# New memory layout for the output projection and the SwiGLU stages, earlier first weights, and squares per tile

## The chip, the cores and the metric

The kernel runs on one core of one Trainium2 chip. The metric is the device time of one execution in microseconds (us). Its median over three executions was 3259.71 us.

## The reference, cut to what matters

The program is one decoder layer over 2048 positions of width 1024, in float32. The parts that matter here come after attention:

```python
merged = g_a * (y_a @ w_proj_a) + g_b * (y_b @ w_proj_b)
x = x + merged @ w_out
h = rms_norm(x, norm_ffn)
x = x + (silu(h @ w_gate) * (h @ w_up)) @ w_down
return rms_norm(x, final_norm)
```

The inner width of the SwiGLU is 2816. `rms_norm` divides each position by the root of its mean square, so it needs a sum of squares over all 1024 features of a position before the first value can be scaled.

## The kernel before

Features lie on the 128 partitions, positions along the free dimension. Every float32 product is made of three fp32r matmuls (`mm3`, lines 161 to 163): a tile is split into a rounded high part (ACT, line 153) and the rest as a low part (DVE or POOL, line 154), and high·high, high·low and low·high are added up in PSUM. A matmul has 128x128 weights and 512 moving columns.

After attention come three stages, each with its own pools, opened one after the other. A pool sits on the left or the right side of the memory, and a tile that lies where an older tile lay waits for the last reader of the older one.

**Stage 3** goes over four groups `j` of 512 positions. For each of eight feature tiles `m`, `project` makes `y_a @ w_proj_a` (PE tile `ppr`, weights `wpr` loaded by SP and split to `wph`, `wpl`), multiplied with a gate (`sg`); the branch b part `mb` is loaded and added by POOL, and split to `mgh` and `mgl`. Then eight rows of the output projection follow (PE tile `po`, line 1070 on, weights `woh`, `wol` which are loaded as `wor` and split once, in j = 0), each of 24 matmuls. DVE adds the residual in `xo`, POOL stores it to `d_x1`, ACT squares it, DVE adds the squares up. `stats` turns the sum into a scale and POOL stores that to `d_rb`. `prep_b` reads `d_x1` and `d_rb` back, makes the right-hand combinations of the seven-product (Strassen) scheme for one pair of feature tiles, and stores them to `d_b`; those of product 1 are kept in `fb0`. It is called at four (j, m) rows.

**Stage 4**, gate and up, makes for two halves of 1024 positions and eleven pairs `p` of weight blocks seven products `i`, in the order 1, 4, 5, 7, 3, 2, 6, each for gate and for up, each of 12 matmuls (PE tile `pgu`). `w_unit` combines the raw weights `fraw` (POOL, tile `cmb`) and splits them (`wfh`, `wfl`); the moving tiles are `fh`, `fl`, read back from `d_b` in the first pass (`load_b`). `store_acts` writes the activations to `d_a`, `prep_down` the combined down weights to `d_w`.

**Stage 5**, down, goes over products 7, 4, 5, 1, 2, 3, 6, each over two halves of the positions and eleven `p`, with four PSUM banks (PE tile `pdn`, 132 matmuls of 512 columns per half). `unit` loads a raw tile and splits it to `uh`, `ul`. `load_acc` loads the residual from `d_x1`; DVE adds each product into it (line 1271). After product 2 and product 6 `final` squares eight tiles one after the other (ACT and DVE), sums over the partitions (`pss`), takes the root, spreads the scale over 512 columns (`dgh`, `dgl`, `pbc`, `rb`), scales eight tiles (line 1244) and stores them.

The order of the instructions on an engine comes from a scheduler that takes the code in program order with a model of durations; within an engine and within the queue of DMAs that it issues, everything goes in that order. SP issues nearly all loads and stores.

## Time and profile before

| what | us |
|---|---|
| median of three executions (lowest 3253.27, highest 3263.06) | 3259.71 |
| the profiled execution | 3251.75 |
| its span | 3250.0 |
| TensorE (PE) busy in the span | 3091.9, 95% |
| VectorE (DVE) busy | 2310.0, 71% |
| ScalarE (ACT) busy | 1433.5, 44% |
| GpSimd (POOL) busy | 1269.9, 39% |

Idle PE time is what there is to gain, since PE is busy nearly everywhere. A row of the waits names who was idle, on which line, and which engine ended that wait. The granted clock (PEclk) is the level that the throttle gave TensorE; 1.00 is 2.4 GHz, and one half is 1.2 GHz.

### The profile page before, as it was taken

How to read it: one execution, taken by the hardware profiler on the slowest of the kernel's cores; microseconds unless marked ns; L12 is line 12 of the kernel's file. 1: busy time of each engine (PE TensorE's matmuls, PEld its weight loads, DVE VectorE, ACT ScalarE, POOL GpSimd, SP SyncE). 2: the span in 40 equal slices, each digit the busy share in tenths (PEclk: the TensorE clock that was granted, in tenths of full speed). 3: DMA queues.
4: the chain of work that ended last, by engine and by line, in shares of the span. 5: the costliest groups of instructions: out<-in, count | busy, mean ns of one | idle time of the engine just before them, and what ended most of it. 6: DMA issues, size and time to landing. Idle time of an engine off the chain costs nothing.

```text
span 3250.0 us, 42942 instructions
## 1 busy us (share of the span) xinstructions
PE 3091.9 (95%) x14434; PEld 2520.4 (78%) x14434; DVE 2310.0 (71%) x4121; ACT 1433.5 (44%) x2687; POOL 1269.9 (39%) x1250
## 2 busy tenths in 40 slices
PE   7999999999899999999899989999999999799998
PEld 6877777777788787888688767888888888688886
DVE  7369998999742888888654757777877666455575
ACT  6434535452344777767421134333533333333342
POOL 3644323352554324233354333333355555331220
PEclk9999999999999999999899989999999999899999
DMA  6424332332553222222466733443644444754453
GB/s 201 113 71 134 106 100 97 119 106 91 205 161 118 77 69 89 73 69 70 149 213 190 272 130 117 140 139 140 230 156 175 156 165 146 262 162 143 135 189 104
DMA packets 249631, 453.32 MB, mean 139 GB/s; under 512 B 35264, under 2 KB 73920, under 8 KB 249280
## 3 DMA queue, kind: packets, MB, share of 16 engines
q1 hardware_dynamic: 231104, 390.78, 36.7%
q0 software_dynamic: 18304, 59.78, 4.9%
q8 instruction: 113, 1.85, 0.2%
q14 instruction: 110, 0.90, 0.1%
HBM read 299.54 MB, written 150.93 MB: 139 GB/s over the span
## 4 chain that ended last, share of the span: by engine, by line
PE 69%; DVE 17%; issue 5%; DMA 3%; ACT 3%; POOL 1%; SPq 0%; DVEq 0%; ACTq 0%; POOLq 0%
PE pgu L162 9%; PE pgu L161 9%; PE pgu L163 9%; PE pdn L161 4%; PE pdn L162 4%; PE pdn L163 4%; DVE X L489 4%; PE ptp L833 3%; DVE y L532 3%; PE pm L161 2%; PE pm L163 2%; PE pm L162 2%; PE O L840 2%; PE O L841 2%; PE pg L161 1%
## 5 line engine op out<-in xcount | busy, mean ns | idle before, releaser
L972 POOL TENSOR_TENSOR cmb<-fraw 128x512 f32<-128x512 f32 x275 | 399.6, 1467 | 473.7 <-DVE wfl L154 454.2
L161 PE MATMUL pgu<-fh,wfh 128*128 128x512 f32 x1232 | 488.6, 398 | 9.5 <-ACT fh L153 5.7
L162 PE MATMUL pgu<-fl,wfh 128*128 128x512 f32 x1232 | 489.8, 398 | 1.8 <-DVE fl L154 1.8
L163 PE MATMUL pgu<-fh,wfl 128*128 128x512 f32 x1232 | 489.0, 398 | 1.7 <-DVE wfl L154 1.7
L161 PEld LDWEIGHTS pgu<-fh,wfh 128*128 128x128 f32 x1232 | 233.1, 189 | 67.1 <-ACT fh L153 7.0
L162 PEld LDWEIGHTS pgu<-fl,wfh 128*128 128x128 f32 x1232 | 233.6, 190 | 59.2 <-DVE fl L154 3.5
L163 PEld LDWEIGHTS pgu<-fh,wfl 128*128 128x128 f32 x1232 | 233.4, 189 | 58.4 <-DVE wfl L154 2.8
L489 DVE SCALAR_TENSOR_TENSOR X<-rl,wi,X 128x512 f32<-128x512 f32 (+3 forms) x266 | 232.1, 882 | 56.9 <-ACT rl L485 43.8
L154 DVE TENSOR_TENSOR wfl<-cmb,wfh 128x512 fp32r<-128x512 f32 x220 | 187.8, 862 | 107.4 <-ACT wfh L153 107.3
L154 DVE TENSOR_TENSOR ul<-raw,uh 128x512 fp32r<-128x512 f32 x154 | 148.1, 969 | 160.9 <-ACT uh L153 160.7
L153 ACT ACTIVATE wfh<-cmb 128x512 fp32r<-128x512 f32 x220 | 138.3, 631 | 264.9 <-PE pgu L162 181.3
L153 ACT ACTIVATE uh<-raw 128x512 fp32r<-128x512 f32 x231 | 137.9, 627 | 253.6 <-PE pdn L163 133.4
L161 PE MATMUL pdn<-uh 128*128 128x512 f32 x616 | 229.6, 391 | 19.1 <-ACT uh L153 19.1
L162 PE MATMUL pdn<-ul,uh 128*128 128x512 f32 x616 | 240.6, 391 | 0.0
L163 PE MATMUL pdn<-uh,ul 128*128 128x512 f32 x616 | 238.6, 390 | 0.0
L161 PE MATMUL pm<-wh,hT 128*128 128x512 f32 (+1 forms) x576 | 223.0, 391 | 12.2 <-ACT wh L153 4.1
L1140 DVE TENSOR_TENSOR s<-s,pgu 128x512 f32<-128x512 f32 x264 | 175.1, 678 | 78.0 <-PE pgu L163 60.1
L485 ACT ACTIVATE rl<-sc 128x512 f32<-128x512 f32 (+3 forms) x304 | 158.6, 549 | 154.9 <-DVE X L489 85.3
L163 PE MATMUL pm<-wh,lT 128*128 128x512 f32 (+1 forms) x576 | 223.6, 389 | 0.0
L162 PE MATMUL pm<-wl,hT 128*128 128x512 f32 (+1 forms) x576 | 223.2, 388 | 0.4 <-POOL wl L154 0.3
L154 POOL TENSOR_TENSOR ul<-raw,uh 128x512 fp32r<-128x512 f32 x77 | 106.6, 1390 | 283.9 <-ACT uh L153 276.1
L153 ACT ACTIVATE pth<-ptp 128x512 fp32r<-128x512 f32 (+1 forms) x320 | 162.3, 532 | 121.3 <-PE ptp L833 112.2
(314 smaller groups left out, 7769.8 us busy)
## 6 DMA issues: line engine op xcount, KB each, us to landing
raw<-d_a SPq DMA_DIRECT2D x154, 256.0 KB, 2.7
wraw<-in_w_in_dram SPq DMA_DIRECT2D x64, 512.0 KB, 4.4
d_a<-cmb SPq DMA_DIRECT2D x110, 256.0 KB, 2.3
fraw<-in_w_gate_dram SPq DMA_DIRECT2D x22, 1024.0 KB, 4.8
fraw<-in_w_up_dram SPq DMA_DIRECT2D x22, 1024.0 KB, 5.0
d_sg<-zg POOLq DMA_DIRECT2D x64, 256.0 KB, 2.6
sg<-d_sg SPq DMA_DIRECT2D x64, 256.0 KB, 3.6
d_w<-cmb SPq DMA_DIRECT2D x55, 256.0 KB, 2.1
```

The lines of the kernel that those rows point to most:

```text
L153: act.activation(h, src, AF.Copy)
L154: lo.tensor_tensor(l, src, _f(h), op=ALU.subtract)
L161: pe.matmul(out, ah, bh, start=first, stop=False, skip_group_check=onto)
L162: pe.matmul(out, ah, bl, start=False, stop=False, skip_group_check=onto)
L163: pe.matmul(out, al, bh, start=False, stop=last, skip_group_check=onto)
L485: act.activation(r[:, :w], sc[:, :w], AF.Relu)
L489: dve.scalar_tensor_tensor(xs, r[:, :w], wi[:, i, h:h + 1], xs, op0=ALU.mult, op1=ALU.add)
L532: dve.tensor_scalar(y, Xs[p], t[:, p:p + 1], None, op0=ALU.is_ge, op1=ALU.add, accum_out=c[:, p:p + 1])
L833: pe.transpose(pt[:, t * P:(t + 1) * P], out["P"][t, kt // 8][:, (kt % 8) * P:(kt % 8 + 1) * P], ident)
L840: pe.matmul(O[:, cs], V, a[:, cs], start=(kt == 0), stop=False)
L972: eng.tensor_tensor(s, blocks[form[0]], blocks[form[1]], op=form[2])
L1140: dve.tensor_tensor(s[to], s[to], b, op=op)
```

## The change

The pools of the three stages are laid out anew. In stage 3 the weights and work tiles go to the right side and `pr_` to the left, the buffers of `mgh` and `mgl` go from 9 to 8, and those of `prep_b` from 8 to 7 in a pool of their own. Stage 4's raw and split weights (`fr`, `fg`) take the place of `pr_`, `cmb` has 2 buffers instead of 3, and the moving tiles get a pool for each product on the right side. Stage 5's raw tiles and split activations lie where product 1's and its neighbours' moving tiles lay, and its split weights alternate between two pools.

Because of that, the first raw weights of gate and up are loaded inside the output projection of j = 3, and `w_unit` for products 1, 4 and 5 is called at the rows m = 1, 2 and 3 there. `prep_b` moves from (2,1), (2,5), (3,1), (3,4) to (2,1), (2,4), (2,6), (3,0). The store to `d_x1` goes from POOL to ACT. In stage 5 each accumulator is squared when it is complete and the square is added into one `sums` tile, and the last half of product 6 is made in two passes of 256 columns, each with a `final` of its own.

```diff
-    pr_, _ = open_pool("pr", 2, side="right", stack=c3r)
-    pp, _ = open_pool("pp", stack=c3)
-    pw, _ = open_pool("pw", 2, stack=c3)
+    pb_, _ = open_pool("pb", side="right", stack=c3)
+    pw, _ = open_pool("pw", 2, side="right", stack=c3)
+    pp, _ = open_pool("pp", side="right", stack=c3)
+    pr_, _ = open_pool("pr", 2, stack=c3r)
...
-        pl, tag = (fb0, f"{k}") if i == 1 else (fbr, f"{i}_{k}")
-        h = pl.tile([P, 512], F32R, name="fh", tag="fh" + tag)
-        l = pl.tile([P, 512], F32R, name="fl", tag="fl" + tag)
+        h = fbp[i].tile([P, 512], F32R, name="fh", tag=f"fh{k}")
+        l = fbp[i].tile([P, 512], F32R, name="fl", tag=f"fl{k}")
         split(h, l, src, dve)
...
-        return pw.tile([P, 512], dt, name=name, tag="pb3", bufs=8)
+        return pb_.tile([P, 512], dt, name=name, tag="pb3", bufs=7)
...
+    c4 = ExitStack()
+    early = {}
+
+    def cmb(name, dt=F32):
+        return fg.tile([P, 512], dt, name=name, tag="cmb", bufs=2)
+
+    def w_unit(blocks, i):
+
+        src = combine(SA[i], blocks, cmb, pool)
+        h = fg.tile([P, 512], F32R, name="wfh", tag="wfh", bufs=6)
+        l = fg.tile([P, 512], F32R, name="wfl", tag="wfl", bufs=6)
+        split(h, l, src, dve)
+        return h, l
+
+    def load_pair(w, p):
+
+        raw = fr.tile([P, 2, D], F32, name="fraw")
+        sp.dma_start(raw, w[2 * p:2 * p + 2].rearrange("f p c -> p f c"))
+        return {(u, v): raw[:, u, v * 512:(v + 1) * 512] for u in range(2) for v in range(2)}
...
-            h = pw.tile([P, 512], F32R, name="mgh", tag="mgh", bufs=9)
-            l = pw.tile([P, 512], F32R, name="mgl", tag="mgl", bufs=9)
+            h = pw.tile([P, 512], F32R, name="mgh", tag="mgh", bufs=8)
+            l = pw.tile([P, 512], F32R, name="mgl", tag="mgl", bufs=8)
...
+        else:
+            c3r.close()
+            fr, _ = open_pool("fr", 3, stack=c4)
+            fg, _ = open_pool("fg", stack=c4)
+            raws = [load_pair(w, 0) for w in (w_gate, w_up)]
         for m in range(KT):
+            if j == 3 and 1 <= m <= 3:
+                i = ORDER[m - 1]
+                for n, raw in enumerate(raws):
+                    early[n, i] = w_unit(raw, i)
...
-            pool.dma_start(d_x1[m * P:(m + 1) * P, rows], xo)
             sq = st_.tile([P, 512], F32, name="sal") if j == 3 and m == KT - 1 else sq3("sq3")
             act.activation(sq, xo, AF.Square)
+            act.dma_start(d_x1[m * P:(m + 1) * P, rows], xo)
...
-            if (j, m) in ((2, 1), (2, 5), (3, 1), (3, 4)):
-                prep_b(0, {(2, 1): 0, (2, 5): 1, (3, 1): 2, (3, 4): 3}[j, m], pb3, keep=(1,))
+            if (j, m) in ((2, 1), (2, 4), (2, 6), (3, 0)):
+                prep_b(0, {(2, 1): 0, (2, 4): 1, (2, 6): 2, (3, 0): 3}[j, m], pb3, keep=(1,))
...
-    fr, _ = open_pool("fr", 3, side="right", stack=c4)
-    fg, _ = open_pool("fg", side="right", stack=c4)
-    fbr, _ = open_pool("fbr", stack=c4)
     fw, _ = open_pool("fw", 2, stack=c4)
+    for i in ORDER[1:]:
+        fbp[i] = open_pool(f"fb{i}", side="right", stack=c4)[0]
...
-            raws = [load_pair(w, p) for w in (w_gate, w_up)]
+            if half or p:
+                raws = [load_pair(w, p) for w in (w_gate, w_up)]
             grp = [Group(), Group()]
             for i in ORDER:
                 if half == 0 and p == 0 and i != 1:
                     load_b(0, i, tmp)
-                for g, raw in zip(grp, raws):
-                    g.product(i, w_unit(raw, i))
+                for n, (g, raw) in enumerate(zip(grp, raws)):
+                    g.product(i, early.pop((n, i), None) or w_unit(raw, i))
...
+    fx, _ = open_pool("fx", side="right", stack=c5)
+    fu, _ = open_pool("fu", side="right", stack=c5)
+    fv = [open_pool(f"fv{u}", side="right", stack=c5)[0] for u in range(2)]
     fa, _ = open_pool("fa", side="right", stack=c5)
-    fx, _ = open_pool("fx", stack=c5)
+    fy, _ = open_pool("fy", 2, stack=c5)
     QN = KT // 2
...
-    def unit(src, kind, bufs, eng):
-        raw = fx.tile([P, 512], F32, name="raw", tag="raw" + kind, bufs=4)
+    def unit(src, pl, kind, bufs, eng):
+        w = src.shape[-1]
+        raw = fx.tile([P, 512], F32, name="raw", tag="raw" + kind, bufs=4)[:, :w]
         sp.dma_start(raw, src)
-        h = fx.tile([P, 512], F32R, name="uh", tag="h" + kind, bufs=bufs)
-        l = fx.tile([P, 512], F32R, name="ul", tag="l" + kind, bufs=bufs)
-        split(h, l, raw, eng)
-        return h, l
+        hl = pl.tile([P, 2, 512], F32R, name="u" + kind, tag="u" + kind, bufs=bufs)
+        split(hl[:, 0, :w], hl[:, 1, :w], raw, eng)
+        return hl[:, 0, :w], hl[:, 1, :w]
 
...
+    def square(half, n, a, c0, w):
+
+        cs = slice(c0, c0 + w)
+        if (half, n) not in sums:
+            sums[half, n] = fy.tile([P, 512], F32, name="sums", bufs=3)
+            act.activation(sums[half, n][:, cs], a[:, cs], AF.Square)
+            return
+        sq = fy.tile([P, 512], F32, name="sq4", bufs=3)
+        act.activation(sq[:, :w], a[:, cs], AF.Square)
+        dve.tensor_tensor(sums[half, n][:, cs], sq[:, :w], sums[half, n][:, cs], op=ALU.add)
+
...
+    def final(half, n, c0, w):
+
+        cs, nt = slice(c0, c0 + w), w // P
+        sa = sums[half, n][:, cs]
         pss = bank("B", "pss4")
-        for t in range(4):
-            pe.matmul(pss[:, t:t + 1], sa[:, t * P:(t + 1) * P], ones[:, 0:1], start=(t == 0), stop=(t == 3))
-        ss = fx.tile([P, 4], F32, name="ss4")
...
+    DONE = {1: (0, 0), 2: (1, 0), 3: (0, 1), 6: (1, 1)}
     seen = set()
+    nw = 0
     for i in (7, 4, 5, 1, 2, 3, 6):
         wu = []
-        for half in range(2):
-            pms = [bank("A", "pdn") for _ in range(QN)]
+        for half, c0, w in ((0, 0, 512), (1, 0, 512)) if i != 6 else ((0, 0, 512), (1, 0, 256), (1, 256, 256)):
...
-                    wu.append(unit(a_src(i, p), "w", 14, pool))
-                bh, bl = unit(d_a[half, i, p], "a", 4, dve)
+                    wu.append(unit(a_src(i, p), fv[nw // 7 % 2], "w", 7, pool))
+                    nw += 1
+                bh, bl = unit(d_a[half, i, p][:, cs], fu, "a", 4, dve)
...
-                    dve.tensor_tensor(a, a, pm, op=op)
+                    dve.tensor_tensor(a[:, cs], a[:, cs], pm, op=op)
+                    if DONE.get(i) == q:
+                        square(half, q[1], a, c0, w)
             if i in (2, 6):
-                final(half, 0 if i == 2 else 1)
+                final(half, 0 if i == 2 else 1, c0, w)
```

On ACT, at the end of the output projection, the program before has the squares of the last rows and then the first split weights; the names `xo` are the result rows, `wfh` the split weights, `s1` a copy of gate or up:

```order
L1075 ACTIVATE sq3_20213<-xo_20184 128x512
L1075 ACTIVATE sal_20245<-xo_20216 128x512
L153 ACTIVATE wfh_20273<-cmb_20271 128x512
L153 ACTIVATE wfh_20294<-cmb_20292 128x512
L153 ACTIVATE wfh_20337<-fraw_20267 128x512
L153 ACTIVATE wfh_20356<-fraw_20269 128x512
L153 ACTIVATE wfh_20401<-cmb_20399 128x512
L153 ACTIVATE wfh_20423<-cmb_20421 128x512
L153 ACTIVATE wfh_20469<-cmb_20467 128x512
L1125 ACTIVATE s1_20290<-pgu_20277 128x512
```

The changed program:

```order
L153 ACTIVATE wfh_20040<-cmb_20038 128x512
L1103 ACTIVATE sq3_19999<-xo_19971 128x512
L1104 DMA d_x1_99<-xo_19971 128x512
L1103 ACTIVATE sq3_20078<-xo_20050 128x512
L1104 DMA d_x1_99<-xo_20050 128x512
L153 ACTIVATE wfh_20046<-cmb_20044 128x512
L153 ACTIVATE wfh_20082<-fraw_19967 128x512
L153 ACTIVATE wfh_20086<-fraw_19969 128x512
L153 ACTIVATE wfh_20124<-cmb_20122 128x512
L1103 ACTIVATE sq3_20118<-xo_20090 128x512
L1104 DMA d_x1_99<-xo_20090 128x512
L153 ACTIVATE wfh_20130<-cmb_20128 128x512
```

The first six `wfh` (products 1, 4, 5, gate and up) now stand between the squares of the rows, and the stores to `d_x1` stand on ACT too.

On SP, at the end of gate and up, the program before has the last stores of the activations, then the loads of the accumulators, then the first raw tiles of the down product:

```order
L1203 DMA acc_28405<-d_x1_99 128x512
L1203 DMA acc_28407<-d_x1_99 128x512
L1203 DMA acc_28655<-d_x1_99 128x512
L1203 DMA acc_28657<-d_x1_99 128x512
L1208 DMA raw_27787<-d_w7_0_17830 128x512
L1208 DMA raw_27793<-d_a0_7_0_17665 128x512
L1208 DMA raw_27811<-d_w7_1_17831 128x512
L1208 DMA raw_27817<-d_a0_7_1_17666 128x512
```

The changed program has these raw loads behind the stores of p = 9, which is one p earlier:

```order
L1162 DMA d_a1_3_9_17765<-cmb_27434 128x512
L1162 DMA d_a1_6_9_17787<-cmb_27438 128x512
L1222 DMA raw_27823<-d_w7_0_17833 128x512
L1222 DMA raw_27828<-d_a0_7_0_17668 128x512
L1222 DMA raw_27845<-d_w7_1_17834 128x512
L1222 DMA raw_27850<-d_a0_7_1_17669 128x512
L1222 DMA raw_27867<-d_w7_2_17835 128x512
L1222 DMA raw_27872<-d_a0_7_2_17670 128x512
```

The accumulators' loads, ahead of the raw loads before, come some 40 rows later.

On DVE, close to the end, the program before has the scaling of half 0's tiles (line 1244) and then the splits of the last p and the additions of the last product:

```order
L1244 SCALAR_TENSOR_TENSOR acc_29405<-acc_29405,gl_112,rb4_31191 128x512
L1244 SCALAR_TENSOR_TENSOR acc_29407<-acc_29407,gl_112,rb4_31191 128x512
L1244 SCALAR_TENSOR_TENSOR acc_29409<-acc_29409,gl_112,rb4_31191 128x512
L1244 SCALAR_TENSOR_TENSOR acc_29411<-acc_29411,gl_112,rb4_31191 128x512
L154 TENSOR_TENSOR ul_31391<-raw_31388,uh_31390 128x512
L154 TENSOR_TENSOR ul_31409<-raw_31406,uh_31408 128x512
L1271 TENSOR_TENSOR acc_29659<-acc_29659,pdn_31222 128x512
L1271 TENSOR_TENSOR acc_29661<-acc_29661,pdn_31223 128x512
L1271 TENSOR_TENSOR acc_29663<-acc_29663,pdn_31224 128x512
L1271 TENSOR_TENSOR acc_29665<-acc_29665,pdn_31225 128x512
```

The changed program, where the pass after it has 256 columns:

```order
L1265 SCALAR_TENSOR_TENSOR acc_28867<-acc_28867,gl_112,rb4_31018 128x512
L1265 SCALAR_TENSOR_TENSOR acc_28869<-acc_28869,gl_112,rb4_31018 128x512
L1265 SCALAR_TENSOR_TENSOR acc_29332<-acc_29332,gl_112,rb4_31018 128x512
L1265 SCALAR_TENSOR_TENSOR acc_29334<-acc_29334,gl_112,rb4_31018 128x512
L1265 SCALAR_TENSOR_TENSOR acc_29336<-acc_29336,gl_112,rb4_31018 128x512
L1265 SCALAR_TENSOR_TENSOR acc_29338<-acc_29338,gl_112,rb4_31018 128x512
L154 TENSOR_TENSOR ua_31315<-raw_31313,ua_31315 128x256
L1296 TENSOR_TENSOR acc_29580<-acc_29580,pdn_31049 128x256
L154 TENSOR_TENSOR ua_31332<-raw_31330,ua_31332 128x256
L1296 TENSOR_TENSOR acc_29582<-acc_29582,pdn_31050 128x256
```

There the eight scalings stand ahead of the split of the second p of the last pass (`ua_31315`).

## Rows read from the trace of the kernel before

**Rows 1.** Windows of the three stages; columns us, PE busy, PEld, DVE, ACT, POOL, PEclk, DMA:
```profile
1597.00:1897.00 300.00, 285.93 (x1255) 232.08 (x1253) 166.79 (x226) 64.70 (x107) 132.95 (x132) 0.97 0.66 219
1897.00:2784.00 887.00, 872.35 (x3706) 700.22 (x3705) 637.08 (x863) 362.02 (x630) 400.64 (x277) 0.99 0.44 154
2784.00:2810.00 26.00, 6.94 (x23) 5.27 (x22) 10.35 (x11) 4.99 (x8) 6.25 (x4) 0.61 0.89 305
```

**Rows 2.** Waits of PE, 1890 to 1942 (us in total, times, longest):
```profile
PE pgu L161 <- ACT fh L153: 5.7, 3, 2.1
PE pgu L161 <- ACT wfh L153: 3.6, 1, 3.6
...
PE pgu L163 <- DVE wfl L154: 1.7, 1, 1.7
```

**Rows 3.** Timeline of POOL and DVE there (start us, us, then the operation):
```profile
1898.85 3.72 POOL L972 TENSOR_TENSOR cmb<-fraw 128x512 f32<-128x512 f32 x3
...
1898.70 4.43 DVE L1077 TENSOR_TENSOR sal<-sal,sq 128x512 f32<-128x512 f32 x1 [0.69 <-ACT sal L1075]
```

**Rows 4.** Window of PE behind that boundary (us, PE busy, PEclk, DMA share, GB/s):
```profile
1896.50:1915.00 18.50, 11.65 (x33) 0.72 0.27 86
```

**Rows 5.** Waits of PE and of ACT, 2783 to 2806:
```profile
PE pdn L161 <- ACT uh L153: 19.1, 1, 19.1
ACT uh L153 <- DMA raw<-d_w: 19.0, 1, 19.0
```

**Rows 6.** Timeline of SP's DMA issues, 2768 to 2804:
```profile
2773.43 8.76 SPq L1203 DMA_DIRECT2D acc<-d_x  x4
...
2796.86 0.32 SPq L1208 DMA_DIRECT2D raw<-d_w  x1
```

**Rows 7.** Timelines of PE, ACT and DVE at the end:
```profile
3230.40 0.39 PE L163 MATMUL pdn<-uh,ul 128*128 128x512 f32 x1
3234.99 1.87 PE L1235 MATMUL pss<-ones,sq 128*128 128x1 f32 x8 [4.20 <-DVE sq L1231]
...
3240.50 0.60 ACT L145 ACTIVATE rb<-pbc 128x512 f32<-128x512 f32 x1 [3.06 <-PE pbc L144]
...
3229.46 2.48 DVE L1271 TENSOR_TENSOR acc<-acc,pdn 128x512 f32<-128x512 f32 x4 [5.29 <-PE pdn L163]
3231.86 3.07 DVE L1231 TENSOR_TENSOR sq<-sq,sq 128x512 f32<-128x512 f32 x4
...
3241.13 5.39 DVE L1244 SCALAR_TENSOR_TENSOR acc<-acc,gl,rb 128x512 f32<-128x512 f32 x8 [1.52 <-ACT rb L145]
```

**Rows 8.** Timeline of PE, matmuls with 256 moving columns:
```profile
858.24 0.28 PE L162 MATMUL pmx<-vl,wsh 128*128 128x256 f32 x1
858.36 0.28 PE L163 MATMUL pmx<-vh,wsl 128*128 128x256 f32 x1
```

**Rows 9.** Waits of PE, 1597 to 1626:
```profile
PE po L162 <- DVE mgl L154: 2.4, 1, 2.4
PE po L161 <- ACT mgh L153: 2.4, 1, 2.4
```

**Rows 10.** Waits of PE, 1785 to 1860:
```profile
PE po L162 <- DVE mgl L154: 2.6, 1, 2.6
PE ppr L161 <- DVE sg L885: 2.5, 1, 2.5
```

**Rows 11.** Page, costliest groups: instructions, busy us, mean ns of one, idle before:
```profile
L972 POOL TENSOR_TENSOR cmb<-fraw 128x512 f32<-128x512 f32 x275 | 399.6, 1467 | 473.7 <-DVE wfl L154 454.2
```

**Rows 12.** Timeline of PE around a change from product 6 to product 1:
```profile
2311.76 0.39 PE L161 MATMUL pgu<-fh,wfh 128*128 128x512 f32 x1
...
2313.17 0.40 PE L161 MATMUL pgu<-fh,wfh 128*128 128x512 f32 x1
...
2315.25 0.39 PE L161 MATMUL pgu<-fh,wfh 128*128 128x512 f32 x1
...
2316.61 0.39 PE L161 MATMUL pgu<-fh,wfh 128*128 128x512 f32 x1
```

More of the change, by code (lines that the diff above doesn't have):

```diff
@@ L1220, in tmp5 @@
     def tmp5(name, dt=F32):
[L1221 to L1245 removed]
+        return fy.tile([P, 512], dt, name=name, tag="tmp", bufs=4)
```

49 lines of the change are left out of this document (16 added, 33 removed).

## The prediction

> **What bounds the kernel now.** I read the busy shares first, then the windows by stage, then PE's waits at each border of two stages, then the timelines of the engines named in these waits. PE is busy 95% of the span, so in the long stretches only the number of matmuls counts, and the change leaves that alone but for the last half of one product. What can be won is idle PE time, and the windows show where it lies: 14 us of 300 in the output projection, 15 us of 887 in gate and up, 19 of the 26 us at the border to the down product [rows 1], and about 20 us behind the last matmul [rows 7]. A long wait is paid twice, since the granted clock is lower for some microseconds behind it: over the 18.5 us that begin at the border to gate and up it is 0.72 [rows 4].
>
> **The change part by part.** The sum is made against the profiled execution's 3251.75 us. The median of the three runs is 8.0 us above that, and the forecast for the median carries these 8.0 us along.
>
> *Border to gate and up.* Before, the first split weights were made only when the last output row was done: POOL combines three tiles in 3.72 us [rows 3], ACT and DVE split, and PE waits 3.6 us for the first high part and 1.7 us for the first low part [rows 2]. The changed order puts six of these splits between the squares of the last rows, many microseconds ahead of their use, so both waits go: 5.3 us. The window there holds 33 matmuls [rows 4], of which I count some 17 at half clock; at 0.2 us more each that is 3.5 us. The three waits for `fh` (5.7 us together [rows 2]) stay: these tiles are still queued on ACT behind the copies of product 1's sums. What is late next is just this, the first `fh` of product 4. I take -9, between -4 (the clock falls all the same, later) and -13 (the `fh` waits shrink too). What is moved ahead must fit into the last rows of the output projection: six ACT splits, six DVE splits, four POOL combinations and two loads of 1 MB. The seven rows after the first last some 38 us (24 matmuls each, 0.227 us apart), which covers all of it, so I cost it at nothing; if that cover were gone it would be about 2 us.
>
> *Border to the down product.* PE waits 19.1 us for a split that itself waits 19.0 us for the first raw tile [rows 5]. The reason stands on SP: the first four accumulator loads take from 2773.43 for 8.76 us, because their places are still in use, and the first raw load is issued only at 2796.86 [rows 6]. In the changed order the raw loads stand ahead of all accumulator loads, on the place of product 1's moving tiles, which are free once product 1 of the last p is done; six more products of 5.6 us follow, so there are some 33 us for a load of under 3 us and for eight splits. On ACT and DVE the first four activation splits come inside the last p, and on POOL the first weight splits do, behind one combination for the last `d_w`. The accumulators come some 40 rows later on SP, and are wanted only after 132 matmuls, about 30 us into the stage. So the wait goes whole, with about 2 us of half clock behind it: -21 at best. What could remain is a microsecond or two because the inserted splits (four of about 1 us on DVE) delay the last weight splits of gate and up. I take -19, between -10 and -21.
>
> The Trainium skill, "SBUF — State Buffer" (section "SBUF: two separate sides"), says that a VectorE operation with two SBUF inputs and a GpSimd operation that reads SBUF take one shared pair of ports in turn, the loser waiting in full. The trace agrees: an addition on DVE took 4.43 us while POOL combined three tiles for 3.72 us [rows 3]. By that rule the four early POOL splits would each hold back DVE in the last p, and this term would come to about -14 instead of -19.
>
> *Attention to projection, and the group changes.* PE waits 4.8 us here for the first `mgh` and `mgl` [rows 9]; the new order fills in ten matmuls of the next projection ahead of the first that need `mgl`, but the splits of `woh` and `wol` now stand ahead of those of the activations on ACT and DVE, which delays the first projection by 1 to 2 us. I take -2, between -6 and +4. At the later group changes the waits of 2.6 and 2.5 us [rows 10] come from gate tiles and splits that are as late as before. There, `mgh` and `mgl` have eight buffers for eight tiles, so none of the next group can be split before the last row's use; against that, the store to `d_x1` no longer sits ahead of POOL's combinations, and `prep_b` is spread otherwise. I take -1, between -9 and +8.
>
> *The end.* From the start of the last matmul to the end of the span are 19.6 us [rows 7]: 4.6 to the sum over partitions (four additions, the chain of squares), 1.9 for that sum, 4.2 to the end of `rb`, 5.4 for eight scalings, 3.5 for the last store. With 256 columns and the squares summed earlier I estimate 2.3 + 1.0 + 2.6 + 3.0 + 3.3 = 12.2, so -7.4. The price is 264 matmuls of 256 columns for 132 of 512: matmuls of that size start 0.12 us apart [rows 8], the large ones 0.227 us, which makes 31.7 against 30.0 us, +1.7. There is a new wait as well: the eight scalings of half 0 (5.39 us [rows 7]) stand on DVE ahead of the split for the second p of the last pass. They can start about 2 us before that pass and end 3.5 us into it, and the split is wanted after 1.7 us; +2.4, perhaps a microsecond more for the clock. In the kernel before a p lasts twice as long and covers this. Together I take -3, between -7 and +2.
>
> *Places of the operands.* In gate and up six matmuls of product 6 take 1.41 us, six of product 1 take 1.36 us [rows 12], which is 0.235 against 0.227 us for one. Product 6's moving tiles lie at the other end of the memory from the weights, product 1's at the same end. For the six products of the first kind (528 matmuls each) this is some 21 us in all. After the change the weights lie low and the moving tiles of products 1, 4, 5 and 7 high, those of 3, 2 and 6 in the middle. If distance is what counts, one or two products gain 3.6 us each and the output projection, whose `mgl` comes to lie far from `woh`, loses 2 to 5. I take 0; the ends are -20 (all at 0.227) and +21 (product 1, the output projection's 768 and the down product's 1848 matmuls all at 0.234).
>
> The Trainium skill, "TensorE: Matmul & The Clock Gate" (section "Step-by-step: what each phase is for"), says that TensorE reads weights and moving columns through two independent ports, so that loading the next weights takes nothing from the running matmul. By it the place would not matter and this term is 0 with no ends; the 0.007 us in the rows is what it doesn't explain.
>
> Sum: -9 - 19 - 2 - 1 - 3 + 0 = -34. From 3251.75 that is 3217.7, and for the median 3259.7 - 34 = 3226.
>
> **The rivals.** (a) *The down product starts late all the same*: the wait moves from the raw load to the POOL splits, which stand behind a combination and in turn with DVE. For it speaks that POOL needs about 1.4 us a split; against it that PE eats a weight tile in 2.7 us and POOL starts some 15 us early. Then only some 5 of 19 us are won: 3259.7 - 20 = 3240. (b) *The places do all the work*: gate and up run at 0.227 us throughout, 20 us more: 3206. Against it speaks that the moving tiles of four products stay far from the weights. (c) *New waits in the projection eat the gain*: with eight buffers, the splits of a group (DVE, close to 0.9 us each) run one behind the other while only the last row's matmuls are there to cover them, 6 us at each of three changes, with 3 us of half clock each: 27 us, so 3253, which is no change. Against it speaks that the order still has matmuls of the next `ppr` between. (d) *Slower*: `cmb` has two buffers instead of three, and every p of gate and up needs ten combinations of 1.467 us [rows 11], each only when the split two before it is done. If PE has to wait in the steady state, it does so in all 22 p; from 1.5 us a p on the whole gain is gone, and 2 us a p gives 44 - 34 = +10: 3270. Against it speaks that POOL has 401 of 887 us there [rows 1], and that six split weights stand between it and PE.
>
> **How the numbers follow.** The forecast has 0.62, with a range of its own from 3205 to 3241; (a) has 0.15, (b) 0.08, (c) 0.09, (d) 0.06. A measurement of this kernel tells 0.3%, about 10 us, from no change. Faster are the forecast, (a) and (b): 0.85; the same is (c): 0.09; slower is (d): 0.06. The range for 8 in 10 leaves out (c), (d) and the lower part of (b): 3200 to 3248.
>
> **What would show it.** The wait of 19.1 us must be gone from PE's waits at the border to the down product, with the first raw loads in the last p of gate and up; if (a) holds, PE waits there for `uw` from POOL. At the border to gate and up the waits for `wfh` and `wfl` must be gone and three for `fh` remain. The span must end some 12 us after the last matmul, with one wait of 2 to 3 us in the pass ahead of it. The distance of the matmuls by product tells about the places. The prediction is wrong if PE's waits in the 880 us of gate and up grow (d), or if those of the projection do (c).

## The result and the profile after

The changed kernel takes 3233.65 us against 3258.0 us for the kernel before (medians), a ratio of 0.9926 with a 95% interval from 0.9903 to 0.995. That is 24 us less; the forecast was 34 less. One of the five executions after took 7833.33 us at a granted clock of 0.394; it is left out of the ratio. The profiled execution after has a span of 3231.1 us, 18.9 under the one before. The table cuts both spans at the first or last matmul of a kind, taken from the starts in the two traces (`O` is a product of attention; the first `pbc` behind the projection, which spreads a scale, comes 216 matmuls into gate and up in all kernels here; differences are taken before rounding):

| stretch, from matmul to matmul (us) | before | after | difference | forecast |
|---|---|---|---|---|
| start to the last `O` of attention (code not changed) | 1597.2 | 1603.8 | +6.7 | 0 |
| to the last `po` (projection) | 299.7 | 301.9 | +2.2 | -3 |
| to the first `pbc` of gate and up (border) | 74.8 | 67.2 | -7.6 | -9 |
| to the last `pgu` (steady gate and up) | 812.8 | 812.3 | -0.4 | 0 |
| to the first `pdn` (border to down) | 19.5 | 0.2 | -19.2 | -19 |
| to the last `pdn` | 426.5 | 432.1 | +5.6 | -3 with the next |
| to the end | 19.7 | 13.5 | -6.2 | see above |

So the two borders came out as forecast, the projection and the end did not, and a stretch that the change doesn't touch moved too. Windows of the stages after (columns as in [rows 1]):

```profile
1604.00:1906.00 302.00, 284.64 (x1252) 229.37 (x1251) 161.94 (x231) 67.59 (x113) 131.32 (x107) 0.98 0.67 214
1906.00:2785.50 879.50, 869.63 (x3707) 697.30 (x3706) 637.57 (x861) 366.68 (x637) 394.94 (x277) 0.99 0.46 160
2785.50:2812.00 26.50, 25.42 (x112) 20.71 (x111) 15.86 (x14) 7.16 (x12) 11.57 (x8) 1.00 0.81 274
```

The third window is the one to compare with [rows 1]: at the border to down PE was busy for 6.94 of 26 us at a granted clock of 0.61, and now is for 25.42 of 26.5 at full clock. The timeline of PE there has no gap, and SP issues the first raw loads 31 us ahead of it, where [rows 6] had the first one at 2796.86, 12 us behind the last `pgu`:

```profile
2785.29 0.39 PE L163 MATMUL pgu<-fh,wfl 128*128 128x512 f32 x1
2785.52 0.40 PE L161 MATMUL pdn<-ua,uw 128*128 128x512 f32 x1
```

```profile
2754.78 0.41 SPq L1222 DMA_DIRECT2D raw<-d_w  x1
2755.28 0.40 SPq L1222 DMA_DIRECT2D raw<-d_a  x1
```

PE's waits at the border to gate and up answer to [rows 2]. Those for `wfh` and `wfl` are gone; the three for `fh` are there to the tenth of a microsecond:

```profile
PE pgu L161 <- ACT fh L153: 5.7, 3, 2.1
PE pgu L162 <- DVE fl L154: 2.7, 2, 1.8
```

The end answers to [rows 7] (timelines of PE, DVE and ACT). The chain has kept its form, and every link but the last store (3.6 us) is shorter; from the last `pdn` at 3217.64 to the end of the span are 13.5 us where 12.2 were estimated:

```profile
3220.39 1.01 PE L1255 MATMUL pss<-ones,sums 128*128 128x1 f32 x4 [2.48 <-DVE sums L1247]
...
3223.85 0.38 ACT L145 ACTIVATE rb<-pbc 128x256 f32<-128x256 f32 x1 [1.92 <-PE pbc L144]
...
3218.33 2.01 DVE L1247 TENSOR_TENSOR sums<-sq,sums 128x256 f32<-128x256 f32 x4
...
3224.27 3.25 DVE L1265 SCALAR_TENSOR_TENSOR acc<-acc,gl,rb 128x256 f32<-128x256 f32 x8 [1.09 <-ACT rb L145]
```

The stall foretold in the last pass is there as well: DVE scales eight tiles of half 0 and only then splits, and PE waits for that split:

```profile
3196.01 5.39 DVE L1265 SCALAR_TENSOR_TENSOR acc<-acc,gl,rb 128x512 f32<-128x512 f32 x8 [0.90 <-ACT rb L145]
3201.32 0.42 DVE L154 TENSOR_TENSOR ua<-raw,ua 128x256 fp32r<-128x256 f32 x1
...
3201.80 0.39 PE L162 MATMUL pdn<-ua,uw 128*128 128x256 f32 x1 [1.67 <-DVE ua L154]
```

**The 6.7 us ahead of the change** are for the most part a matter of the granted clock. PE's timelines show the same instructions in the same order. At 1224 us, in both executions, PE waits 1.42 us for `Pt` and 1.21 us for `pth`, and then, in the one before, goes on at 0.23 us a matmul:

```profile
1224.00 0.55 PE L833 MATMUL ptp<-ident,Pt 128*128 128x128 f32 x3 [1.42 <-ACT Pt L822]
1225.75 0.50 PE L840 MATMUL O<-pth,V 128*128 128x512 f32 x1 [1.21 <-ACT pth L153]
1226.09 0.40 PE L161 MATMUL ppr<-yth,wph 128*128 128x512 f32 x1
1226.33 0.40 PE L162 MATMUL ppr<-ytl,wph 128*128 128x512 f32 x1
```

and in the one after at 0.43 us, the half clock, for a dozen matmuls:

```profile
1225.84 0.55 PE L833 MATMUL ptp<-ident,Pt 128*128 128x128 f32 x3 [1.42 <-ACT Pt L822]
1227.59 0.79 PE L840 MATMUL O<-pth,V 128*128 128x512 f32 x1 [1.21 <-ACT pth L153]
1228.18 0.63 PE L161 MATMUL ppr<-yth,wph 128*128 128x512 f32 x1
1228.61 0.63 PE L162 MATMUL ppr<-ytl,wph 128*128 128x512 f32 x1
```

That makes 2.7 us here, and the same at 1377 us makes 2.8; the other 1.2 us are many small differences. Over the profiles of this study in which this part has the same instructions at the same addresses, the last `O` starts between 1595.5 and 1604.3 us, so a single profile holds some 9 us of chance there, and the stretches are compared rather than the spans. The clock is not the whole of that chance: the profile with 1604.3 us waits 5.4 us longer near 345 us than the one before. Without this stretch the profile shows 25.6 us less, which agrees with the 24 us between the medians.

### The profile page after: what moved, and what is told of

The parts are those of the page before. It is cut to its first block, busy times and chain, and to the rows that moved or that the text cites. A ratio compares the mean times of both kernels' runs of the same rounds, so it can differ in the third digit from the quotient of the medians.

```text
span 3231.1 us, 43210 instructions
## 1 busy us (share of the span) xinstructions
PE 3092.3 (96%) x14568; PEld 2524.1 (78%) x14568; DVE 2280.8 (71%) x4150; ACT 1437.2 (44%) x2704; POOL 1254.7 (39%) x1218
## 4 chain that ended last, share of the span: by engine, by line
PE 68%; DVE 18%; DMA 5%; issue 4%; ACT 3%; POOL 1%; SPq 0%; DVEq 0%; ACTq 0%; POOLq 0%
PE pgu L163 9%; PE pgu L162 9%; PE pgu L161 9%; DVE X L489 4%; PE pdn L161 4%; PE pdn L162 4%; PE pdn L163 4%; DVE y L532 4%; PE ptp L833 3%; PE O L840 2%; PE pm L161 2%; PE pm L162 2%; PE pm L163 2%; PE O L841 2%; PE ppr L161 1%
## 5 line engine op out<-in xcount | busy, mean ns | idle before, releaser
L162 PE MATMUL pdn<-ua,uw 128*128 128x512 f32 (+1 forms) x660 | 247.5, 376 | 2.7 <-DVE ua L154 2.7
L163 PE MATMUL pdn<-ua,uw 128*128 128x512 f32 (+1 forms) x660 | 245.3, 375 | 0.0
L154 DVE TENSOR_TENSOR ua<-raw,ua 128x512 fp32r<-128x512 f32 (+1 forms) x165 | 119.8, 731 | 175.9 <-ACT ua L153 175.8
L161 PE MATMUL pdn<-ua,uw 128*128 128x512 f32 (+1 forms) x660 | 239.6, 376 | 1.5 <-ACT ua L153 1.3
L154 POOL TENSOR_TENSOR uw<-raw,uw 128x512 fp32r<-128x512 f32 x77 | 107.6, 1406 | 262.9 <-ACT uw L153 234.4
L161 PE MATMUL pg<-hT,wh 128*128 128x512 f32 x512 | 203.2, 397 | 6.8 <-ACT zg L449 6.8
```

What stands on the lines that cost most here:

```text
L154: lo.tensor_tensor(l, src, _f(h), op=ALU.subtract)
L161: pe.matmul(out, ah, bh, start=first, stop=False, skip_group_check=onto)
L162: pe.matmul(out, ah, bl, start=False, stop=False, skip_group_check=onto)
L163: pe.matmul(out, al, bh, start=False, stop=last, skip_group_check=onto)
```

## Experiments

In each table cell below a stretch is cut as in the table above.

| kernel | projection | border | steady gate and up | border to down | down | end | ratio to before |
|---|---|---|---|---|---|---|---|
| before | 299.7 | 74.8 | 812.8 | 19.5 | 426.5 | 19.7 | |
| after | 301.9 | 67.2 | 812.3 | 0.2 | 432.1 | 13.5 | 0.9926 |
| splits not early | 303.6 | 69.2 | 812.6 | 0.2 | 432.1 | 13.5 | 0.9936 |
| accumulators' pool first | 303.0 | 69.0 | 812.8 | 7.8 | 439.5 | 13.1 | 0.9977 |
| last half in one pass | 302.5 | 67.2 | 812.3 | 0.2 | 426.6 | 19.6 | 0.9937 |
| weights among the moving tiles | 302.9 | 72.8 | 792.5 | 0.2 | 436.1 | 12.8 | 0.9892 |
| 32 bytes of padding | 304.9 | 67.1 | 799.3 | 0.2 | 432.7 | 13.0 | 0.9894 |
| low parts on POOL | 305.8 | 67.4 | 812.3 | 0.2 | 430.4 | 12.8 | 0.9928 |
| `prep_b` at its old rows | 304.8 | 67.4 | 812.3 | 0.2 | 432.5 | 12.9 | 0.9936 |
| store on POOL | 310.1 | 68.8 | 812.5 | 0.2 | 432.4 | 13.5 | 0.9948 |
| among them, shifted 32 bytes | 300.1 | 72.7 | 812.6 | 0.2 | 431.2 | 13.1 | 0.9949 |
| all together | 297.1 | 68.3 | 792.3 | 0.2 | 430.2 | 12.8 | 0.9853 |
| all together, eight buffers | 295.6 | 66.6 | 792.5 | 0.2 | 431.4 | 12.8 | 0.9843 |
| before, 32 bytes of padding | 298.1 | 75.0 | 810.8 | 19.4 | 426.5 | 19.6 | 0.9999 |

Four kernels with the same code and addresses in the projection (after, accumulators first, one pass, low parts on POOL) give 301.9 to 305.8 us there, so a difference of 4 us in that column shows nothing. The columns of the borders, gate and up and the end repeat within 2 us, mostly within 0.5.

**The early splits undone**

```diff
-            if j == 3 and 1 <= m <= 3:
-                i = ORDER[m - 1]
-                for n, raw in enumerate(raws):
-                    early[n, i] = w_unit(raw, i)
```

> The changed kernel with its six early weight splits made at the start of gate and up again (loads and places as changed). Theory (the early splits give the gain at that border): the waits of PE for wfh (3.6 us) and wfl (1.7 us) come back and the half clock behind them; from the last output matmul to the first pbc of gate and up it takes 72 to 73 us as before, not 65.3, and the output projection stays at 302 us. Rival (the early splits cost the projection what they give at the border): the projection falls below 300 us and the sum of both stretches stays at 367 us.

The border grew by 2.0 us, not by 7, and neither of the two waits came back; the rival is wrong too, as the projection didn't get shorter. The timeline of POOL tells why: without the calls, the first combinations still ran inside the projection, 20 to 30 us before its end at 1899.6, because their tiles' places (those of `pr_`) were free and the scheduler put them there.

```profile
1869.50 3.06 POOL L973 TENSOR_TENSOR cmb<-fraw 128x512 f32<-128x512 f32 x2 [2.79 <-DMA fraw<-in_w_up_dram]
1873.19 1.68 POOL L973 TENSOR_TENSOR cmb<-fraw 128x512 f32<-128x512 f32 x1 [0.63 <-DVE wfl L154]
1876.10 1.68 POOL L973 TENSOR_TENSOR cmb<-fraw 128x512 f32<-128x512 f32 x1 [1.23 <-DVE wfl L154]
```

Even the 2.0 us are not shown to be the calls'. PE's waits in this stretch come to 8.4 us with them and without; what differs is the granted clock, and the run with the accumulators' pool first (below), which has the calls, shows the same. PE in this stretch, after, without the calls, and with the accumulators first (us, PE busy, PEclk, DMA share, GB/s):

```profile
1905.70:1972.90 67.20, 57.38 (x227) 0.92 0.44 150
1899.50:1968.70 69.20, 59.42 (x227) 0.90 0.43 146
1898.40:1967.40 69.00, 59.19 (x226) 0.90 0.43 147
```

So of the 7.6 us at this border no part is shown to come from the calls. The two runs with the split weights on the place of the projection's tiles (below) have no early splits either and stand at 72.7 and 72.8 us: there POOL's first combination starts at 1904.22, when the projection is over, and a wait of 2.1 us for `wfh` is back. The place of the split weights is thus worth some 3.6 us against the run without calls; the 2 us from 72.8 to 74.8 come with other parts of the change and were not separated.

**The accumulators' pool first again**

```diff
+    fa, _ = open_pool("fa", side="right", stack=c5)
     fx, _ = open_pool("fx", side="right", stack=c5)
     fu, _ = open_pool("fu", side="right", stack=c5)
     fv = [open_pool(f"fv{u}", side="right", stack=c5)[0] for u in range(2)]
-    fa, _ = open_pool("fa", side="right", stack=c5)
```

> The changed kernel with one line moved: the accumulators' pool of the down product is opened first again, so that the raw tiles lie on the places of later products' moving tiles. Theory (the gain at the border to the down product comes from where the raw tiles lie, which sets when SP can issue their loads): the wait between the last pgu and the first pdn comes back, 8 to 20 us instead of 0.23. Rival (it comes from the order of the code or the separate pools alone): it stays under 2 us.

One line moved brings back 15 us of waiting, 7.5 ahead of the first `pdn`, just under the 8 expected at the least, and 7.3 at a weight tile 20 us later (PE's waits there):

```profile
PE pdn L161 <- ACT uw L153: 14.8, 2, 7.5
```

So the order of the places is the cause for 15 of the 19.2 us won here. With the line moved, the accumulators lie where products 1, 4, 5 and 7 had their moving tiles and the raw tiles where products 7 and 3 had theirs; SP then issues the first accumulator load at 2761.52 and the first raw load only at 2769.73, some 11 us ahead of the last `pgu` instead of 31. Whether it takes the raw tiles' place or the accumulators' loads ahead of them was not separated, and neither was what makes the remaining 4 us.

**The last half in one pass**

```diff
-        for half, c0, w in ((0, 0, 512), (1, 0, 512)) if i != 6 else ((0, 0, 512), (1, 0, 256), (1, 256, 256)):
+        for half, c0, w in ((0, 0, 512), (1, 0, 512)):
```

> The changed kernel with the last half of product 6 in one pass of 512 columns again; the squares stay summed tile by tile. Theory (the 256-column passes gain at the end but pay with slots and a stall): the end behind the last matmul grows from 13.5 to 16.5 to 18 us, the down stretch shrinks from 432.1 by 3 to 6 us, and the two nearly cancel, within 2 us. Rival (the split is a gain of several us): the sum of down stretch and end grows by 4 us or more.

The end grew by 6.1 us and the down stretch shrank by 5.5, which is a difference of 0.6: the two nearly cancel, as the theory has it, though the end grew past its 16.5 to 18 us. The two passes are worth next to nothing. The sums tile by tile alone give nothing at the end either, 19.6 against 19.7 us: PE's wait there is still 4.2 us long, just as in [rows 7], since the last four squares and their additions come behind the last product in either form.

```profile
PE pss L1255 <- DVE sums L1247: 4.2, 1, 4.2
```

**Low parts of the last passes on POOL**

```diff
-                bh, bl = unit(d_a[half, i, p][:, cs], fu, "a", 4, dve)
+                bh, bl = unit(d_a[half, i, p][:, cs], fu, "a", 4, pool if w == 256 else dve)
```

> The changed kernel with the low parts of the activations of the two 256-column passes made by POOL instead of DVE. Theory (the stalls in the last passes come from the eight scalings of half 0 that stand on DVE ahead of a split): PE's waits of 1.7 us and more for ua in the last pass go and the down stretch is 2 to 5 us shorter than 432.1. Rival (they come from the loads or from ACT): unchanged within 1 us.

PE's waits for DVE's `ua` fall from 2.7 to 0.7 us, and the one of 1.7 us in the last pass is gone; the stretch is 1.7 us shorter (the end, 0.7 shorter, is within what it repeats to). The theory names the right wait, and the wait was smaller than the 2 to 5 us expected.

**The projection: `prep_b` at its old rows, and the store on POOL**

```diff
-            if (j, m) in ((2, 1), (2, 4), (2, 6), (3, 0)):
+            if (j, m) in ((2, 1), (2, 5), (3, 1), (3, 4)):
```

> The changed kernel with prep_b at its old rows (2,1), (2,5), (3,1), (3,4). Theory (the projection grew by 2 to 4 us because three of four preparations now meet in j = 2, with loads that hold DVE up): the projection falls from 302 to 303.5 us by 2 us or more. Rival (the order at its start or the eight buffers of mgh and mgl): it stays at 302 us or more.

No change, as the rival has it: 304.8 us lies among those of the changed kernel. The rows of `prep_b` are not what cost the projection its time.

```diff
-            act.dma_start(d_x1[m * P:(m + 1) * P, rows], xo)
+            pool.dma_start(d_x1[m * P:(m + 1) * P, rows], xo)
```

> The changed kernel with the store of the output rows on POOL's queue again. Theory (the store ahead of POOL's combinations held them back at the border to gate and up only because their places were taken as well): the border stays within 1 us of 67.2 us and the projection within 1.5 us of 302. Rival (the queue of the store gives several us of the gain at the border): the border grows by 2 us or more.

The border stayed within 1.6 us, but the projection came to 310.1 us, 4 to 8 above the others: both expectations were wrong about where it shows. POOL's waits in the projection suggest how it may come about. The store stands in POOL's order and waits there for DVE's result, 21 times, and POOL's weight splits and `mb` additions queue behind it:

```profile
POOL d_x L1104 <- DVE xo L1101: 82.6, 21, 6.1
```

That this is what reaches PE is not shown, since POOL waits in the changed kernel too, there 72.8 us for PE. So the move of the store to ACT, which I had priced together with `prep_b` at -1, is worth 4 to 8 us in this one profile, which is of the slowest of four executions (3243.01 us). The medians are 3236.75 us here, and in the same session 3234.28 with `prep_b` at its old rows, so the size is open. If it is a gain at all, something else in the layout must cost as much or more.

**Where the operands of gate and up lie.** Four runs ask why a matmul of gate and up takes 0.234 us with one place of the operands and 0.227 us with another [rows 12]. In the first, the split weights come to lie among the moving tiles, without early splits:

```diff
-            fg, _ = open_pool("fg", stack=c4)
...
     for i in ORDER[1:]:
+        if i == 3:
+            fg, _ = open_pool("fg", side="right", stack=c4)
         fbp[i] = open_pool(f"fb{i}", side="right", stack=c4)[0]
```

> As the run without early splits, but the split weights of gate and up lie among the moving tiles, at 132 to 160 KB, and all moving tiles at 84 to 224 KB. Theory (a matmul whose weights and moving tile lie in far apart parts of the memory takes 0.006 us longer): the matmuls of gate and up start 0.2275 us apart instead of 0.2333, for at least five of seven products, and the stage is 15 to 21 us shorter than without early splits. Rival (two independent read ports, place does not matter): 0.233 us and no difference.

All seven products run at 0.2268 us and the stage is 20.1 us shorter than without early splits. The theory's numbers came; its reason, the distance, does not survive the next runs. In the timeline, six matmuls take 1.36 us:

```profile
2300.15 0.39 PE L161 MATMUL pgu<-fh,wfh 128*128 128x512 f32 x1
...
2301.51 0.39 PE L161 MATMUL pgu<-fh,wfh 128*128 128x512 f32 x1
```

The second pads the left side and leaves everything else where it is:

```diff
     cp = ctx.enter_context(tc.tile_pool(name="const", bufs=1))
+    cp.tile([P, 8], F32, name="pad")
```

> The changed kernel with 32 bytes of padding ahead of all that lies on the left side of the memory; nothing else. Every run so far fits two readings: two tiles of one matmul lie in far parts of the memory, or their addresses differ modulo 64 (left-side pools begin at 0 modulo 64, right-side pools at 32). Theory (the address modulo 64 decides): with the padding all tiles begin at 32 modulo 64, so the matmuls of gate and up start 0.227 us apart although the weights stay at 46 to 70 KB, and the stage is about 20 us shorter. Rival (the distance decides): 0.233 us as in the changed kernel, no difference.

32 bytes took 13.1 us off the stage, at 0.2291 us a matmul, with the weights as far away as before. Distance alone is not the cause, then; but the padding does not win the whole 20 us either. The third sets the weights among the moving tiles and shifts them by 32 bytes (and with the second pad the moving tiles of products 3, 2 and 6 by 64):

```diff
+            sh = [open_pool(f"sh{n}", side="right", stack=c4)[0] for n in range(1)]
+            sh[0].tile([P, 8], F32, name="sh0")
             fg, _ = open_pool("fg", side="right", stack=c4)
+            sh.append(open_pool("sh1", side="right", stack=c4)[0])
+            sh[1].tile([P, 8], F32, name="sh1")
```

> As the run with the weights among the moving tiles, but the weights' pool moved by 32 bytes, so that weights begin at 0 and moving tiles at 32 modulo 64. It is the fourth case of two by two: near and equal gave 0.2268 us from matmul to matmul, far and equal 0.229, far and unequal 0.2333. Theory (the address modulo 64 and the place both count, one on top of the other): near and unequal gives 0.231 us, and the steady part of gate and up is 807 us or a little less. Rival (only being far apart lets the address count): 0.227 us and 793 us.

Here all products are back at 0.2333 us and the stage at 812.6 us; in the timeline six matmuls take 1.40 us:

```profile
2302.09 0.40 PE L161 MATMUL pgu<-fh,wfh 128*128 128x512 f32 x1
...
2303.49 0.40 PE L161 MATMUL pgu<-fh,wfh 128*128 128x512 f32 x1
```

Both my expectations were wrong, the one that the effects add (0.231) and the one that near tiles don't care (0.227). 32 bytes decide over the full 20 us among near tiles, and over 13.1 us where the weights lie far away. The last pads the kernel before:

```diff
     cp = ctx.enter_context(tc.tile_pool(name="const", bufs=1))
+    cp.tile([P, 8], F32, name="pad")
```

> The kernel before with the 32 bytes of padding on the left and nothing else. Theory (addresses that differ modulo 64 cost 0.006 us a matmul wherever they meet; equal ones cost nothing with weights in the upper part of the memory): the six products of gate and up that ran 0.234 us apart run at 0.227 to 0.228, steady gate and up falls from 812.8 to 793 to 796 us, and the kernel is 15 to 20 us faster with the borders unchanged (74.8 and 19.5 us). Rival (it needs the other layout as well): under 5 us.

2 us in the stage, and a ratio of 0.9999 (0.9986 to 1.0013): wrong again, though the addresses of all operands in gate and up are equal modulo 64 (the rival's "under 5 us" came). So modulo 64 is not the rule. With the addresses modulo 128 of the moving tiles and the weights, as the programs place them, the cases fall into place:

| kernel, products | moving | weights | us a matmul |
|---|---|---|---|
| before, product 1 | 96 | 96 | 0.2277 |
| before, the other six | 0 | 96 | 0.2342 |
| after, all | 96 | 0 | 0.2333 |
| weights among the moving tiles | 96 | 96 | 0.2268 |
| the same, shifted 32 bytes | 32 or 96 | 64 | 0.2333 |
| 32 bytes of padding | 96 | 32 | 0.2291 |
| before, 32 bytes of padding, product 1 | 96 | 96 | 0.2276 |
| before, 32 bytes of padding, the other six | 32 | 96 | 0.2333 |
| all together | 96 | 96 | 0.2268 |
| down product, before and after | 0; 96 | 0; 96 | 0.2269 |

In every row in which both are equal modulo 128 the matmuls run 0.227 to 0.228 us apart, and in every row in which they differ it is 0.229 to 0.234. Operands that are equal modulo 128 here are equal modulo 256 and 512 too, so these are not told apart. This rule was read out of all these runs together and has no run of its own; a padding of 96 bytes, which would make the left side of the kernel before equal to the right, was not tried. Why 64 bytes one way cost 0.0023 us and the other way 0.0065 stays open. Matmuls of the same shape in attention, outside the table, follow it in part (medians over those without a wait): `pm` in the kernel before stands at 0.227 us with its operands at 0 and 0 and at 0.234 with them at 0 and 96, but `sc` stands at 0.233 with 0 and 32 and, with the padding, at 0.234 with 32 and 32. So it is not shown as a rule for all matmuls.

**All together**

```diff
+    cp.tile([P, 8], F32, name="pad")
...
-    pb_, _ = open_pool("pb", side="right", stack=c3)
-    pw, _ = open_pool("pw", 2, side="right", stack=c3)
-    pp, _ = open_pool("pp", side="right", stack=c3)
-    pr_, _ = open_pool("pr", 2, stack=c3r)
+    pr_, _ = open_pool("pr", 2, side="right", stack=c3r)
+    pp, _ = open_pool("pp", stack=c3)
+    pw, _ = open_pool("pw", 2, stack=c3)
+    pb_, _ = open_pool("pb", stack=c3)
...
-            fr, _ = open_pool("fr", 3, stack=c4)
-            fg, _ = open_pool("fg", stack=c4)
+            fg, _ = open_pool("fg", side="right", stack=c4)
+            fr, _ = open_pool("fr", 2, side="right", stack=c4)
...
+    frb, _ = open_pool("frb", stack=c4)
...
     fx, _ = open_pool("fx", side="right", stack=c5)
+    fa, _ = open_pool("fa", side="right", stack=c5)
     fu, _ = open_pool("fu", side="right", stack=c5)
     fv = [open_pool(f"fv{u}", side="right", stack=c5)[0] for u in range(2)]
-    fa, _ = open_pool("fa", side="right", stack=c5)
```

> All together: 32 bytes of padding on the left, the split weights of gate and up at 180 to 206 KB on the right (on the place that the projection's tiles leave, so that they can still be made early), the moving tiles at 65 to 161 KB and at 207 to 223, nine buffers of mgh and mgl again, the raw and split tiles of the down product on early products' places and the accumulators on the weights' place, and POOL splits in the last passes. Theory (the gains add up): steady gate and up 793 to 799 us, border 67 to 68 us, border to down under 2 us, projection not above 302 us, in all 3210 to 3220 us. Rival (the places get in each other's way again): a wait of 5 us or more at the border to the down product, or gate and up at 812 us.

3203.78 us against 3251.69, a ratio of 0.9853 (0.9836 to 0.9869): better than both kernels, by 1.5% and, going by the two ratios, about 0.7%. The stretches came out as expected, none more than 0.7 us past its bound, with the projection at 297.1 us, and the whole is 6 us under the expected range. (Its diff leaves out what stands above or below: nine buffers, the POOL splits, and a counter that lets every third raw tile go to `frb`.) With eight buffers of `mgh` and `mgl` instead of nine:

```diff
-            h = pw.tile([P, 512], F32R, name="mgh", tag="mgh", bufs=9)
-            l = pw.tile([P, 512], F32R, name="mgl", tag="mgl", bufs=9)
+            h = pw.tile([P, 512], F32R, name="mgh", tag="mgh", bufs=8)
+            l = pw.tile([P, 512], F32R, name="mgl", tag="mgl", bufs=8)
```

> The version with all together, but with eight buffers of mgh and mgl as in the changed kernel; nothing else. Theory (rival (c) of the prediction: with eight buffers for eight tiles the projection waits more at its group changes): the projection grows from 297.1 us to 300 us or more, with the part of the second group (j = 1) above 64 us as in the changed kernel. Rival (what cost the projection there is the other things that the change moved, the places of pr_ and the weights of the projection): it stays at 297 to 298 us and j = 1 at 60.5.

3203.74 us, a ratio of 0.9843 (0.9821 to 0.9864), and a projection of 295.6 us: the rival is right, and the ninth buffer is worth nothing in this layout. The windows of its stages, to compare with those of after:

```profile
1598.00:1894.00 296.00, 283.40 (x1254) 229.77 (x1254) 164.00 (x231) 67.78 (x113) 128.46 (x107) 0.98 0.68 218
1894.00:2755.00 861.00, 849.64 (x3717) 698.41 (x3716) 640.64 (x862) 361.52 (x635) 399.36 (x276) 0.99 0.47 163
```

Gate and up has the same 3696 matmuls. PE is busy 20.0 us less in it and idle 1.5 us more (11.4 against 9.9), which makes the 18.5 us between the windows.

## Why the prediction was right, and where not

**Direction and size.** Faster, and by 24 us where 34 were forecast; the time lies in the forecast's own range. The forecast's way (a set of waits at the stage borders goes, the long stretches stay) is what happened, and of the difference of 10 us the stretches show 8, nearly all of it in three terms: the border to gate and up, the projection and the end.

**Border to the down product, -19: right,** the term and, for most of it, the cause. The run with the accumulators first shows the order of the places to be the cause for 15 of the 19.2 us. Rival (a) fell: PE has no wait for POOL's `uw` there. The estimate of -14 that followed from the Trainium skill, "SBUF — State Buffer" (section "SBUF: two separate sides"), by which POOL's and DVE's splits hold each other up, did not come true: the term was -19.2 and PE has no wait at the border, so whatever turns the two took cost PE nothing there.

**Border to gate and up, -9: nearly right, with the wrong reason for a part.** It was -7.6, both named waits went and the three for `fh` stayed. But I credited the new position of the six splits, and the run without it has the same waits of PE; the place of the split weights gives some 3.6 us, and the rest was not separated. The step that failed is the reading of the order: here a unit's position in it followed from when its memory was free, and not from the code's position.

**Projection, -3: wrong.** It was +2.2 in this profile, and up to +6 in others of the same code. The failed steps are the -2 for its start and the -1 for the group changes. PE's waits at the start answer to [rows 9]: the waits for `mgh` and `mgl` fell from 4.8 to 2.1 us as foretold, and in their place those ahead of the first projection grew, for `ytk` from the DMAs, `ytl` and `wph` (the first two lines are before, the others after):

```profile
PE pty L869 <- DVE ytl L154: 1.0, 1, 1.0
PE ppr L161 <- POOL wph L150: 0.8, 1, 0.8
...
PE pty L869 <- DMA ytk<-d_ya: 2.1, 3, 1.1
PE po L161 <- ACT mgh L153: 1.8, 1, 1.8
PE ppr L161 <- POOL wph L150: 1.8, 2, 0.9
PE pty L869 <- DVE ytl L154: 1.6, 1, 1.6
...
PE po L162 <- DVE mgl L154: 0.3, 1, 0.3
```

I had seen that the splits of the output weights move ahead and priced it at 1 to 2 us; it was 4.6 us to the first `po` (18.8 before, 23.3 after), with 10.2 us at half clock instead of 3.4. Most of that is made up again before the group ends: cut at the last `po` of each, the four groups of positions took 90.9, 60.6, 83.4 and 64.8 us before, and 90.6, 66.5, 82.7 and 62.2 after. They don't hold the same work, though. The new order runs 126, 73, 125 and 60 `ppr` matmuls in them, the one before 132, 60, 132 and 60. The windows of the second group with `ppr` alone, before and after:

```profile
1688.10:1748.70 60.60, 14.68 (x60) 1.00 0.55 177
1694.40:1760.90 66.50, 17.88 (x73) 1.00 0.54 175
```

At about 0.23 us a matmul, an estimate from these counts, the start cost 1.1 us instead of winning 2. Of the 5.9 us that the second group grew by, 3.0 are the 13 matmuls that moved into it and 2.0 are waits of PE, where it had none before; the last group won 2.6. In the second group DVE waits for `prep_b`'s load with the splits `ytl` and `mgl` behind it; its waits for these loads over the projection, before and after:

```profile
DVE x1s L997 <- DMA x1s<-d_x: 18.8, 6, 6.7
DVE x1s L997 <- DMA x1s<-d_x: 24.7, 9, 7.4
```

This wait is not shown to be the cause, since the version with all together has 17.8 us of it with eight buffers and no gap of PE in that group. What the runs do show: it is not the rows of `prep_b`, not the number of buffers (tried in the layout of all together alone; rival (c), a loss of 27 us, did not come), and not the store's move to ACT, since the projection was no shorter with the store on POOL. In the version with all together, where the projection's weights and work tiles lie on the left and `pr_` on the right as before the change, the start takes 20.0 us to the first `po` and the second group 60.5, with 60 `ppr` in it again. Which tile's place makes the difference was not tried, so the cause stays open.

**The end, -3: the mechanism right, the sizes off.** The chain fell by 6.2 instead of 7.4 us, and the price was 5.5 instead of 4.1: 1.7 for the smaller matmuls and 1.7 for the foretold stall are accounted for, and of the rest 0.5 us is PE's wait for the sums between the passes; the other 1.6 us are open. Together -0.6 instead of -3.

**Places of the operands, 0: right in sum by luck, wrong in the picture.** Gate and up changed by -0.4 us, because six products went from 0.2342 to 0.2333 us and product 1 from 0.2277 to 0.2333, which happens to cancel. Distance, on which I had let the bounds rest, is not what counts: a product whose tiles lie at 110 KB and one at 208 KB run alike, and 32 bytes turn the effect on among near tiles. The 20 us named as rival (b) are real, and the version with all together takes them. The rule of two independent read ports (Trainium skill, "TensorE: Matmul & The Clock Gate", section "Step-by-step: what each phase is for"), from which I had taken that the place would not matter, disagrees in this with the runs: the stage takes 792 or 812 us with the same matmuls, and the measurement decides.

**Rival (d)** (waits in the steady state because of two `cmb` buffers) fell: 812.3 against 812.8 us.

## What to carry to other kernels

Where a scheduler sets the order, look up which old tile a new tile lies on: its last reader decides when the load can start, and moving a pool can be worth more than moving code (15 us for one line here). When matmuls of the same shape have two distances in one profile, compare the addresses of their moving tiles and weights, here modulo 128 bytes, before looking for a wait; in this kernel 20 us hung on them, and no view of waits shows it, since the engine is busy either way. And compare profiles by stretches: the part ahead of the change differed by up to 9 us between executions of the same instructions.

## What was not expected of the hardware

- In gate and up and in the down product, the distance of fp32r matmuls with 512 columns and new weights each time is 0.2268 to 0.2278 us or 0.2291 to 0.2342 us, by the addresses of the two operands. Shifting the weights' pool by 32 bytes moved a stage of 3696 matmuls from 792.5 to 812.6 us.
- After the same waits of 1.42 and 1.21 us, the granted clock fell to a half in one execution (matmuls 0.43 us apart) and stayed full in another (0.23 us apart).
